# Splitting a state-space group at its scan, and a third weight buffer, in a hybrid encoder trunk

## The chip, the cores and the metric

The kernel runs on one core of a Trainium2 chip. The metric is the device time of one execution in microseconds (us); less is better. The program is built by a scheduler that fixes the order of instructions on each engine ahead of time; at run time each engine goes through its own list and waits on semaphores.

## The reference

One layer of an encoder on 3072 rows of 1024 columns (a sequence of 1024 and one of 2048), in float32. Cut to what matters:

```python
h = rmsnorm(x, norm_g);  proj = h @ w_in
u_a, v_a, z_a, x_b, z_b = split(proj)                 # five blocks of 1024 columns
y_a = gelu(u_a) * (w_s (x) layernorm(gelu(v_a)) + b_s) * silu(z_a)   # mixing in chunks of 128 rows
y   = s5_forward(x_b) + s5_backward(x_b) + d_skip * x_b    # 64 groups of 16 channels, 64 complex states
gy  = gelu(y);  gy = gy * sigmoid(gy @ w_glu + b_glu);  y_b = gy * silu(z_b)
out = rmsnorm(x + concat(y_a, y_b) @ w_out)
```

## The kernel before

All large products are made of float32 split into a high and a low part, three matmuls for each pair of tiles (`mm3`, lines 57 to 61): high by high, high by low, low by high. The rows are handled as three thirds (`th`) of 1024, each as two halves of 512 columns (`jh`).

There are four stages. The first (to 392 us) makes the block x_b for all thirds and the matrices of the S5 groups. The second (to 1727 us) makes the other four blocks of the input projection, third 2 first, then 0, then 1. The third makes the GLU product of the S5 branch in six halves, and the fourth the output projection.

In the second stage a third runs as follows. Four column blocks of v (`v_part`, line 506), each in four parts of 48 short matmuls into `acc`, with the layer norm statistics behind the last of them. Then eight feature blocks of z_b (`zb_op`), each in two half-steps of 24 matmuls, with eight matmuls of the mixing (`sv`) after each half-step. Then u and z_a by turns, 32 half-steps. A half-step's result leaves its PSUM buffer in two operations: a tanh or gelu on ScalarE (L541, L580), then a product on VectorE (L542, L582). Five PSUM buffers (tag `mm`) are shared by these and the mixing.

The weights of a sweep are in a tile `whl` of 1 MB. In third 2 it is loaded as float32 and split by ScalarE (L151) and GpSimd (L152), and stored; in the other thirds it is loaded ready made (`whl<-wc_d`, L146). The pool has two buffers. `next_w` asks for another one when the second half of a sweep is traced.

After each half-step or v part, `advance` (line 418) may take up to one more piece of the S5 generator `s5_groups` (line 1028): 128 pieces over 184 of these places, two pieces to a group. What a piece issues on ScalarE and on VectorE is queued behind the last eviction (`tail["S"]`, `tail["V"]`), which the gates of z_b, z_a and u set for both and the v parts for ScalarE alone; what it issues on TensorE isn't tied to anything.

The first piece of group g is `states(g)`: six matmuls `pb` (L59 to L61), two products with the cosine and sine table (L1108, L1109), a sum and a difference (L1110, L1111) into tile `b`, two scans over 64 partitions each (L1116), two products back (L1121, L1122), and four more operations (L1123 to L1126) that leave the states `h` in a high and a low part; then `prepare(g + 1)`, which splits that group's input `u` and matrices `mi` and `mo` (ScalarE at L1051; VectorE or GpSimd at L1052), and for two groups at once the angle tables (`tables`, `finish_tables`). The second piece is `outputs(g - 1)`: nine matmuls `py` and a gelu; then `decay(g + 1)` and `issue(g + 2)`, four loads on the SP queue. Tiles `h` and `mi` have two buffers; `u` and `mo` have three.

When the last group is done, `preload` gets the first two rows of `w_glu` and all eight tiles of the first GLU half (`gf`, `gh`) into the space that the groups used.

Of the kernel before, what the change touches and what calls it, by code (L numbers as in the profile page):

```python
# [21 lines left out]
P = 128  # L22
D = 1024
KT = 8
# [32 lines left out]
def mm3(nc, out, lh, ll, rh, rl, first, last):  # L57

    nc.tensor.matmul(out, lh, rh, start=first, stop=False)  # L59
    nc.tensor.matmul(out, lh, rl, start=False, stop=False)  # L60
    nc.tensor.matmul(out, ll, rh, start=False, stop=last)  # L61


def hybrid_encoder(ctx, tc, a, outs):
# [54 lines left out]

    halves, ready, staged = {}, [], []  # L120


# [16 lines left out]
    def split_w(hp):  # L139

        with tc.high_priority(offset=hp):
            if staged:
                n, wfs, view = staged.pop(0)
                w = wpool.tile([P, 2, KT, P], F32R, tag="whl", name="whl")
                if wfs is None:
# [36 lines left out]
    def sweep(pool, half, ops, after, hp=WHP):  # L182

        ws = [ready.pop(0) for _ in ops]
        for jh in range(2):
            for w, f in zip(ws, ops):
                ps = pool.tile([P, 512], F32, tag="mm", name="mm")
                h = half(jh)
                for kt in range(KT):
                    mm3(nc, ps, w[:, 0, kt], w[:, 1, kt], h[kt][:, 0], h[kt][:, 1], kt == 0, kt == KT - 1)  # L190
                if jh:
                    next_w(hp)
                f(jh, ps)
                after()
# [173 lines left out]
    with ExitStack() as p2:  # L368
# [6 lines left out]
        ps_b = p2.enter_context(tc.tile_pool(name="ps_b", bufs=1, space=PSUM))  # L375

        s5 = s5_groups(tc, spool, ps_b, small, kio, f8h, f8l, r8, xb_d, ks_d, mat_d, gy_d)
        done = [0, 0]
# [5 lines left out]
        def preload():  # L384
# [5 lines left out]
            elif len(wg) < 4:  # L390
# [7 lines left out]
                wg.append(w)  # L398
            elif len(g0) < KT:
                for kt in (len(g0), len(g0) + 1):  # L400
                    gf = wg[1].tile([P, 512], F32, name=f"gf{kt}")
                    dma(quad(gf), gy_half(0, kt))
                    gh = wg[1].tile([P, 2, 512], F32R, name=f"gh{kt}")
                    S.copy(gh[:, 0], gf)
                    V.tensor_tensor(gh[:, 1], gf, gh[:, 0].bitcast(F32), op=ALU.subtract)
                    g0.append((gf, gh))

        late = [[], []]
        tail = {}

# [40 lines left out]
        for th in (2, 0, 1):  # L451
# [53 lines left out]
            def v_part(acc, w, cb, q, jh):  # L505

                for cc in range(2):
                    ps = acc[jh][cc]
                    for i in range(2):
                        csl = slice(P * (2 * cc + i), P * (2 * cc + i) + P)  # L510
                        for t in range(4):
                            h, wh, wl = hs[jh][4 * q + t], w[:, 0, 2 * t:2 * t + 2], w[:, 1, 2 * t:2 * t + 2]

                            mm3(nc, ps[:, i], h[:, 0, csl], h[:, 1, csl], wh, wl, q == t == i == 0, q == i == 1 and t == 3)
                    if q:
# [112 lines left out]
    for kt in range(2, KT):  # L628
        wg.append(load_rows(a["w_glu"][0][P * kt:P * kt + P], wresB, yp, "f2k", 9))
    for kt in range(KT):  # L630
        z = e32t("z")
        dma(quad(z), zb_half(0, kt))
# [397 lines left out]
def s5_groups(tc, sp, ps, small, kio, f8h, f8l, r8, xb_d, ks_d, mat_d, gy_d):  # L1030
# [23 lines left out]
    def tables(g):  # L1054

        tb = sp.tile([P, 2, 2, KK], F32, tag="tab", name="tab", bufs=2)
        for q in range(2):
            sc, fr = f8h[:, g + q:g + q + 1], tb[:, q, 0]
            tmp = tb[:, q, 1]
            S.activation(tmp, kio, AF.Copy, scale=sc, bias=MAGIC)  # L1060
            S.activation(tmp, tmp, AF.Copy, bias=-MAGIC)
            V.scalar_tensor_tensor(fr, kio, sc, tmp, op0=ALU.mult, op1=ALU.subtract)
            V.scalar_tensor_tensor(fr, kio, f8l[:, g + q:g + q + 1], fr, op0=ALU.mult, op1=ALU.add)
        V.tensor_scalar(tb[:, :, 0], tb[:, :, 0], 0.5, -0.5, op0=ALU.min, op1=ALU.max)
        st["tab", g], st["tab", g + 1] = tb[:, 0], tb[:, 1]
        st["pair", g] = tb

    def finish_tables(g):
        tb = st.pop(("pair", g))
        S.activation(tb[:, :, 1], tb[:, :, 0], AF.Sin, scale=TWO_PI_LOW)  # L1070
        S.activation(tb[:, :, 0], tb[:, :, 0], AF.Abs)
        S.activation(tb[:, :, 0], tb[:, :, 0], AF.Sin, scale=-TWO_PI_LOW, bias=qpi)

# [13 lines left out]
    def prepare(g):  # L1087
        U, m1, m2 = st.pop(("raw", g))
        u = sp.tile([P, 2, KK], F32R, tag="u", name="u", bufs=3)
        mi = sp.tile([P, 2, 2, P], F32R, tag="mi", name="mi", bufs=2)  # L1090
        mo = sp.tile([P, 2, 3, P], F32R, tag="mo", name="mo", bufs=3)
# [3 lines left out]
        st[g] = u, mi, mo  # L1095

    def states(g):
        u, mi, mo = st[g]
        tb = st.pop(("tab", g))
        cs = tb[:, 0:1].to_broadcast(sh)  # L1100
        sn = tb[:, 1:2].to_broadcast(sh)

# [11 lines left out]
        for r, o, z in ((slice(0, 64), gp[:, 2:2 * KK + 2], (0, P)), (slice(64, 128), gp[:, 0:2 * KK], (P - 1, KK - 1))):  # L1114
            f = slice(None, None, 1 if r.start == 0 else -1)
            V.tensor_tensor_scan(o[r, f], dec[r, f], bf[r, f], 0.0, op0=ALU.mult, op1=ALU.add)  # L1116
            V.memset(gt[r, :, z[0]:z[1] + 1:z[1] - z[0]], 0.0)
        h = sp.tile([P, 2] + sh[1:], F32R, tag="h", name="h", bufs=2)
        h1 = sp.tile(sh, F32, tag="b1", name="h1")
# [33 lines left out]
    issue(0)  # L1153
    tables(0)
    prepare(0)
    finish_tables(0)
    decay(0)
    issue(1)
# [51 lines left out]
```

## Time and profile before

| what | value |
|---|---|
| median of 3 runs | 2536.09 us (2534.43 to 2537.3) |
| the profiled execution | 2535.16 us, of it a span of 2533.3 us |
| TensorE (matmul) busy | 2443.2 us of the span |
| VectorE busy | 1748.9 us |
| ScalarE busy | 959.0 us |
| GpSimd busy | 622.0 us |
| mean granted TensorE clock | 0.989 |

Busy time of TensorE is the union of its matmuls, which overlap one another in the pipeline, so a busy TensorE isn't one at its peak. A wait is idle time of an engine, put down to the instruction that ended it.

### The profile page before, as it was taken

How to read it: one execution, taken by the hardware profiler on the slowest of the kernel's cores; microseconds unless marked ns; L12 is line 12 of the kernel's file. 1: busy time of each engine (PE TensorE's matmuls, PEld its weight loads, DVE VectorE, ACT ScalarE, POOL GpSimd, SP SyncE). 2: the span in 40 equal slices, each digit the busy share in tenths (PEclk: the TensorE clock that was granted, in tenths of full speed). 3: DMA queues.
4: the chain of work that ended last, by engine and by line, in shares of the span. 5: the costliest groups of instructions: out<-in, count | busy, mean ns of one | idle time of the engine just before them, and what ended most of it. 6: DMA issues, size and time to landing. Idle time of an engine off the chain costs nothing.

```text
span 2533.3 us, 33967 instructions
## 1 busy us (share of the span) xinstructions
PE 2443.2 (96%) x12313; PEld 2080.2 (82%) x12313; DVE 1748.9 (69%) x2921; ACT 959.0 (38%) x1698; POOL 622.0 (25%) x623
## 2 busy tenths in 40 slices
PE   7899999989999899999999999999999999999998
PEld 5677779977888898888889788887888888888887
DVE  6898857899999979888887999764334433333332
ACT  5343334445554534444454444423223311111110
POOL 2579873344334302210130221001000200000000
PEclk9999999999999999999999999999999999999999
DMA  8565455445555533444453344455656632222220
GB/s 241 174 190 146 143 164 178 134 152 163 185 179 195 175 109 115 146 154 150 136 177 118 112 140 143 145 162 171 166 155 174 216 108 88 96 96 96 96 75 34
DMA packets 363017, 367.21 MB, mean 145 GB/s; under 512 B 40768, under 2 KB 308576, under 8 KB 350560
## 3 DMA queue, kind: packets, MB, share of 16 engines
q1 hardware_dynamic: 311008, 343.99, 43.0%
q10 hardware_dynamic: 51840, 21.04, 3.4%
q8 instruction: 97, 1.59, 0.3%
q14 instruction: 72, 0.59, 0.1%
HBM read 229.76 MB, written 135.20 MB: 144 GB/s over the span
## 4 chain that ended last, share of the span: by engine, by line
PE 69%; DVE 17%; POOL 3%; DMA 3%; issue 2%; ACT 1%; SPq 0%; ACTq 0%; DVEq 0%; POOLq 0%
PE mm L59 19%; PE mm L61 19%; PE mm L60 19%; DVE gt L1116 3%; PE acc L59 2%; PE acc L61 2%; PE acc L60 2%; DVE h L1122 1%; PE py L59 1%; PE py L61 1%; PE py L60 1%; DVE h L1121 1%; DVE v L479 1%; DMA hf<-hs_d 1%; PE s5b L1002 1%
## 5 line engine op out<-in xcount | busy, mean ns | idle before, releaser
L59 PE MATMUL mm<-w,yh 128*128 128x512 f32 x768 | 302.6, 394 | 0.0
L60 PE MATMUL mm<-w,yh 128*128 128x512 f32 x768 | 301.8, 393 | 0.0
L61 PE MATMUL mm<-w,yh 128*128 128x512 f32 x768 | 301.3, 392 | 0.0
L59 PE MATMUL mm<-hb,whl 128*128 128x512 f32 x704 | 278.3, 395 | 0.0
L59 PE MATMUL mm<-ha,whl 128*128 128x512 f32 x704 | 277.4, 394 | 0.9 <-DVE ha L287 0.8
L61 PE MATMUL mm<-ha,whl 128*128 128x512 f32 x704 | 275.4, 391 | 1.1 <-POOL whl L152 1.1
L60 PE MATMUL mm<-hb,whl 128*128 128x512 f32 x704 | 276.3, 393 | 0.0
L61 PE MATMUL mm<-hb,whl 128*128 128x512 f32 x704 | 276.3, 392 | 0.0
L60 PE MATMUL mm<-ha,whl 128*128 128x512 f32 x704 | 275.6, 391 | 0.0
L1116 DVE TENSOR_TENSOR_SCAN gt<-dec,b 64x768 f32<-64x768 f32 x128 | 230.8, 1803 | 3.1
L152 POOL TENSOR_TENSOR whl<-wf,whl 128x512 fp32r<-128x512 f32 x112 | 175.3, 1581 | 222.2 <-ACT whl L151 192.8
L1052 POOL TENSOR_TENSOR mi<-m,mi 128x256 fp32r<-128x256 f32 x64 | 60.9, 952 | 531.4 <-ACT mi L1051 531.4
L61 PEld LDWEIGHTS mm<-w,yh 128*128 128x128 f32 x768 | 144.3, 188 | 33.7
L59 PEld LDWEIGHTS mm<-w,yh 128*128 128x128 f32 x768 | 144.1, 188 | 33.2
L60 PEld LDWEIGHTS mm<-w,yh 128*128 128x128 f32 x768 | 144.2, 188 | 33.0
L695 DVE SCALAR_TENSOR_TENSOR yh<-yf,yh 128x512 fp32r<-128x512 f32 x96 | 66.8, 699 | 147.8 <-ACT yh L694 110.3
L724 DVE TENSOR_TENSOR xr<-xr,mm 128x512 f32<-128x512 f32 x48 | 33.0, 687 | 184.1 <-PE mm L61 184.1
L61 PEld LDWEIGHTS mm<-ha,whl 128*128 128x128 f32 x704 | 132.9, 189 | 29.5 <-POOL whl L152 1.6
L61 PEld LDWEIGHTS mm<-hb,whl 128*128 128x128 f32 x704 | 133.5, 190 | 28.2
L59 PEld LDWEIGHTS mm<-ha,whl 128*128 128x128 f32 x704 | 132.7, 189 | 27.1 <-DVE ha L287 1.5
L59 PEld LDWEIGHTS mm<-hb,whl 128*128 128x128 f32 x704 | 133.9, 190 | 25.5 <-DVE v L503 0.2
L60 PEld LDWEIGHTS mm<-hb,whl 128*128 128x128 f32 x704 | 133.8, 190 | 25.6 <-DVE hb L288 0.2
(243 smaller groups left out, 5922.3 us busy)
## 6 DMA issues: line engine op xcount, KB each, us to landing
whl<-wc_d SPq DMA_DIRECT2D x64, 1024.0 KB
wc_d<-whl SPq DMA_DIRECT2D x32, 1024.0 KB
wf<-in_w_in_dram SPq DMA_DIRECT2D x112, 256.0 KB
m<-mat_d SPq DMA_DIRECT2D x128, 128.0 KB
xb_d<-xo SPq DMA_DIRECT2D x24, 512.0 KB
U<-xb_d SPq DMA_DIRECT2D x64, 192.0 KB
gy_d<-gy SPq DMA_DIRECT2D x64, 192.0 KB
zb_d<-zb SPq DMA_DIRECT2D x24, 512.0 KB
```

The lines of the kernel that those rows point to most:

```text
L59: nc.tensor.matmul(out, lh, rh, start=first, stop=False)
L60: nc.tensor.matmul(out, lh, rl, start=False, stop=False)
L61: nc.tensor.matmul(out, ll, rh, start=False, stop=last)
L152: G.tensor_tensor(flat[:, 1, sl], wf, flat[:, 0, sl].bitcast(F32), op=ALU.subtract)
L479: V.tensor_scalar(v, v, rs[:, q:q + 1], nb[:, q:q + 1], op0=ALU.mult, op1=ALU.add)
L695: V.scalar_tensor_tensor(y[:, 1], yf, sc, y[:, 0].bitcast(F32), op0=ALU.mult, op1=ALU.subtract)
L724: V.tensor_tensor(x, x, t.ps[i], op=ALU.add)
L1002: T.matmul(pk[:, g], bm[:, i, g], pcl[i][:, g].rearrange("p j c -> p (j c)"), start=i == 0, stop=i == 1)
L1052: eng.tensor_tensor(t[:, 1], src, t[:, 0].bitcast(F32), op=ALU.subtract)
L1116: V.tensor_tensor_scan(o[r, f], dec[r, f], bf[r, f], 0.0, op0=ALU.mult, op1=ALU.add)
L1121: V.tensor_tensor(h1, gt, cs, op=ALU.mult)
L1122: V.tensor_tensor(h2, gt[:, ::-1], sn, op=ALU.mult)
```

## The change

A group's first piece now ends at the scan; the rest of the old `states` is a function `turn(g)` in the second piece, behind `outputs(g - 1)`. The preparation of the next group, its tables (half of a pair at a time) and the finishing of a pair move from the first piece to the second; `issue(g + 1)` stands at the end of the first piece in place of `issue(g + 2)` at the end of the second. `tail["T"]` holds the last matmul of a half-step or v part, so that the pieces' matmuls are queued behind it. `finish_tables` makes both angles first and then one Sin over both. Tiles `mi` and `h` have one buffer. The weights get a third buffer, a pool of its own in the second stage, taken by turns with the two others. To make room at the end of that stage, four of the eight `gf` tiles go through a staging tile, and are loaded a second time at the start of the GLU stage.

```diff
     halves, ready, staged = {}, [], []
+    pools = [wpool]
+    tail = {}
...
-                w = wpool.tile([P, 2, KT, P], F32R, tag="whl", name="whl")
+                w = pools[0].tile([P, 2, KT, P], F32R, tag="whl", name="whl")
+                pools.append(pools.pop(0))
...
+                    tail["T"] = mm3(nc, ps, w[:, 0, kt], w[:, 1, kt], h[kt][:, 0], h[kt][:, 1],
+                                    kt == 0, kt == KT - 1)
...
+        pools[:] = [p2.enter_context(tc.tile_pool(name="wpool3", bufs=1)), wpool, wpool]
+        next_w()
...
+                raw = stage_tile("gf").rearrange("p (a c) -> p a c", a=2) if len(g0) > 3 else None
                 for kt in (len(g0), len(g0) + 1):
-                    gf = wg[1].tile([P, 512], F32, name=f"gf{kt}")
+                    gf = wg[1].tile([P, 512], F32, name=f"gf{kt}") if kt < 4 else raw[:, kt % 2]
...
+                            tail["T"] = mm3(nc, ps[:, i], h[:, 0, csl], ...)     # in v_part
...
     for kt in range(KT):
+        if kt > 3:
+            g0[kt][0] = f32t("gf")
+            dma(quad(g0[kt][0]), gy_half(0, kt))
         z = e32t("z")
...
     def tables(g):
-        tb = sp.tile([P, 2, 2, KK], F32, tag="tab", name="tab", bufs=2)
-        for q in range(2):
-            ...
-        V.tensor_scalar(tb[:, :, 0], tb[:, :, 0], 0.5, -0.5, op0=ALU.min, op1=ALU.max)
+        if g % 2 == 0:
+            tb = sp.tile([P, 2, 2, KK], F32, tag="tab", name="tab", bufs=2)
+            ...
+        V.tensor_scalar(fr, fr, 0.5, -0.5, op0=ALU.min, op1=ALU.max)
     def finish_tables(g):
         tb = st.pop(("pair", g))
-        S.activation(tb[:, :, 1], tb[:, :, 0], AF.Sin, scale=TWO_PI_LOW)
+        S.activation(tb[:, :, 1], tb[:, :, 0], AF.Copy, scale=-1.0, bias=0.25)
         S.activation(tb[:, :, 0], tb[:, :, 0], AF.Abs)
-        S.activation(tb[:, :, 0], tb[:, :, 0], AF.Sin, scale=-TWO_PI_LOW, bias=qpi)
+        flat = tb.rearrange("p q i k -> p (q i k)")
+        S.activation(flat, flat, AF.Sin, scale=-TWO_PI_LOW, bias=qpi)
...
-        mi = sp.tile([P, 2, 2, P], F32R, tag="mi", name="mi", bufs=2)
+        mi = sp.tile([P, 2, 2, P], F32R, tag="mi", name="mi")
...
             V.memset(gt[r, :, z[0]:z[1] + 1:z[1] - z[0]], 0.0)
-        h = sp.tile([P, 2] + sh[1:], F32R, tag="h", name="h", bufs=2)
+    def turn(g):
+        u, mi, mo = st[g]
+        cs, sn = phase(g)
+        h = sp.tile([P, 2] + sh[1:], F32R, tag="h", name="h")
...
         states(g)
         store()
         if g < GRP - 1:
-            prepare(g + 1)
-        if g % 2 == 0 and g < GRP - 2:
-            tables(g + 2)
-        if g % 2 == 1 and g < GRP - 1:
-            finish_tables(g + 1)
+            issue(g + 1)
         yield
         if g:
             outputs(g - 1)
+        if g % 2 and g < GRP - 1:
+            tables(g + 2)
+        if g < GRP - 1:
+            prepare(g + 1)
+        turn(g)
+        if g % 2 and g < GRP - 1:
+            finish_tables(g + 1)
+        if g % 2 == 0 and g < GRP - 2:
+            tables(g + 2)
         if g < GRP - 1:
             decay(g + 1)
-        if g < GRP - 2:
-            issue(g + 2)
-        if g == GRP - 1:
+        else:
```

## Rows read from the trace of the kernel before

**Rows 1.** The page: the span, and VectorE's busy time, share and instructions.

```profile
span 2533.3 us, 33967 instructions
PE 2443.2 (96%) x12313; PEld 2080.2 (82%) x12313; DVE 1748.9 (69%) x2921; ACT 959.0 (38%) x1698; POOL 622.0 (25%) x623
```

**Rows 2.** TensorE's waits in the second stage: waiter, releaser, total us, times, longest.

```profile
PE sv L498 <- DVE zb L542: 23.5, 9, 5.8
PE acc L59 <- DMA whl<-wc_d: 11.0, 4, 7.5
PE acc L59 <- ACT hb L444: 2.2, 1, 2.2
```

**Rows 3.** Windows: length, PE, PEld, DVE, ACT, POOL busy, clock, DMA share, GB/s.

```profile
498.00:643.00 145.00, 129.60 (x622) 111.31 (x621) 141.35 (x194) 73.35 (x141) 67.16 (x47) 0.94 0.51 162
643.00:840.00 197.00, 197.00 (x907) 167.85 (x906) 189.61 (x235) 102.40 (x169) 75.45 (x52) 1.00 0.56 184
959.00:1090.00 131.00, 124.61 (x619) 107.38 (x618) 120.89 (x194) 65.78 (x124) 34.74 (x28) 0.99 0.44 138
1400.00:1533.00 133.00, 126.54 (x622) 108.96 (x621) 120.84 (x189) 67.14 (x125) 34.84 (x28) 0.97 0.43 135
```

**Rows 4.** Windows at half clock in the second stage (seven of them), and their sum.

```profile
842.80:853.00 10.20, 4.63 (x22) 4.67 (x23) 6.92 (x9) 4.82 (x10) 5.51 (x4) 0.50 0.76 275
sum 37.40, PE 26.98 PEld 24.16 DVE 33.64 ACT 19.80 POOL 16.09; mean PE 3.85 PEld 3.45 DVE 4.81 ACT 2.83 POOL 2.30
```

**Rows 5.** Timeline of VectorE at 1440 us: start, us, engine, line, operation, tiles.

```profile
1440.46 0.95 DVE L1122 TENSOR_TENSOR h<-gt,tab 128x768 f32<-128x768 f32 x1
1441.33 0.68 DVE L542 SCALAR_TENSOR_TENSOR zb<-zb,mm 128x512 f32<-128x512 f32 x1
```

**Rows 6.** Windows of tiles b and h alone; lines of VectorE in the second stage.

```profile
385.00:1690.00 1305.00, 423.67 (x384) 0.99 0.46 150
385.00:1690.00 1305.00, 78.46 (x384) 68.71 (x384) 327.15 (x384) 0.99 0.46 150
L1062 DVE SCALAR_TENSOR_TENSOR tab<-kio,f8h,tab 128x384 f32<-128x384 f32 x61 | 44.5, 733 | 1.5 <-ACT tab L1061 0.6
L1052 DVE TENSOR_TENSOR u<-U,u 128x384 fp32r<-128x384 f32 x62 | 37.6, 607 | 24.5 <-PE pb L61 21.0 <-ACT u L1051 3.5
```

**Rows 7.** Timelines of the SP queue and of VectorE at the change of thirds.

```profile
841.69 0.36 SPq L440 DMA_DIRECT2D hf<-hs_d  x1
842.15 0.42 SPq L146 DMA_DIRECT2D whl<-wc_d  x1
...
840.94 0.68 DVE L445 TENSOR_TENSOR ha<-hf,ha 128x512 fp32r<-128x512 f32 x1
...
864.84 0.68 DVE L445 TENSOR_TENSOR hb<-hf,hb 128x512 fp32r<-128x512 f32 x1
```

**Rows 8.** Timelines of TensorE and VectorE: pb, and the gate of the half-step before.

```profile
614.61 0.39 PE L59 MATMUL pb<-u,mi 128*128 128x384 f32 x1
...
614.62 0.68 DVE L542 SCALAR_TENSOR_TENSOR zb<-zb,mm 128x512 f32<-128x512 f32 x1
...
1571.33 0.34 PE L59 MATMUL pb<-u,mi 128*128 128x384 f32 x1
...
1569.05 0.68 DVE L582 TENSOR_TENSOR v<-v,mm 128x512 f32<-128x512 f32 x1
```

**Rows 9.** Timelines of VectorE and GpSimd: one operation beside GpSimd, and alone.

```profile
500.55 1.65 DVE L1111 TENSOR_TENSOR b<-b,b 128x384 f32<-128x384 f32 x1
...
498.94 2.84 POOL L152 TENSOR_TENSOR whl<-wf,whl 128x512 fp32r<-128x512 f32 x2
...
827.82 0.55 DVE L1111 TENSOR_TENSOR b<-b,b 128x384 f32<-128x384 f32 x1
```

**Rows 10.** Timelines of the SP queue and of TensorE at the GLU's start.

```profile
1748.98 6.89 SPq L643 DMA_DIRECT2D gf<-gy_d  x8
...
1761.60 0.50 PE L59 MATMUL mm<-gh,w 128*128 128x512 f32 x1 [0.60 <-ACT t L674]
```

**Rows 11.** Lines of ScalarE in the second stage: the second Sin of a pair.

```profile
L1072 ACT ACTIVATE tab<-tab,qpi 128x768 f32<-128x768 f32 x31 | 29.1, 939 | 0.9
```

More of the change, by code (lines that the diff above doesn't have):

```diff
@@ L60, in mm3 @@
     nc.tensor.matmul(out, lh, rl, start=False, stop=False)
-    nc.tensor.matmul(out, ll, rh, start=False, stop=last)
+    return nc.tensor.matmul(out, ll, rh, start=False, stop=last)
 def hybrid_encoder(ctx, tc, a, outs):
@@ L189, in sweep @@
                 for kt in range(KT):
-                    mm3(nc, ps, w[:, 0, kt], w[:, 1, kt], h[kt][:, 0], h[kt][:, 1], kt == 0, kt == KT - 1)
+                    tail["T"] = mm3(nc, ps, w[:, 0, kt], w[:, 1, kt], h[kt][:, 0], h[kt][:, 1],
+                                    kt == 0, kt == KT - 1)
                 if jh:
@@ L405, in preload @@
                     V.tensor_tensor(gh[:, 1], gf, gh[:, 0].bitcast(F32), op=ALU.subtract)
-                    g0.append((gf, gh))
+                    g0.append([gf, gh])
         late = [[], []]
-        tail = {}
+        tail.clear()
         def flush():
@@ L512, in v_part @@
                             h, wh, wl = hs[jh][4 * q + t], w[:, 0, 2 * t:2 * t + 2], w[:, 1, 2 * t:2 * t + 2]
-                            mm3(nc, ps[:, i], h[:, 0, csl], h[:, 1, csl], wh, wl, q == t == i == 0, q == i == 1 and t == 3)
+                            tail["T"] = mm3(nc, ps[:, i], h[:, 0, csl], h[:, 1, csl], wh, wl, q == t == i == 0, q == i == 1 and t == 3)
                     if q:
@@ L1054, in tables @@
     def tables(g):
-        tb = sp.tile([P, 2, 2, KK], F32, tag="tab", name="tab", bufs=2)
-        for q in range(2):
[L1058 to L1063, printed above, removed]
-        V.tensor_scalar(tb[:, :, 0], tb[:, :, 0], 0.5, -0.5, op0=ALU.min, op1=ALU.max)
-        st["tab", g], st["tab", g + 1] = tb[:, 0], tb[:, 1]
-        st["pair", g] = tb
+        if g % 2 == 0:
+            tb = sp.tile([P, 2, 2, KK], F32, tag="tab", name="tab", bufs=2)
+            st["tab", g], st["tab", g + 1] = tb[:, 0], tb[:, 1]
+            st["pair", g] = tb
+        sc, tb = f8h[:, g:g + 1], st["tab", g]
+        fr, tmp = tb[:, 0], tb[:, 1]
+        S.activation(tmp, kio, AF.Copy, scale=sc, bias=MAGIC)
+        S.activation(tmp, tmp, AF.Copy, bias=-MAGIC)
+        V.scalar_tensor_tensor(fr, kio, sc, tmp, op0=ALU.mult, op1=ALU.subtract)
+        V.scalar_tensor_tensor(fr, kio, f8l[:, g:g + 1], fr, op0=ALU.mult, op1=ALU.add)
+        V.tensor_scalar(fr, fr, 0.5, -0.5, op0=ALU.min, op1=ALU.max)
     def finish_tables(g):
         tb = st.pop(("pair", g))
-        S.activation(tb[:, :, 1], tb[:, :, 0], AF.Sin, scale=TWO_PI_LOW)
+        S.activation(tb[:, :, 1], tb[:, :, 0], AF.Copy, scale=-1.0, bias=0.25)
         S.activation(tb[:, :, 0], tb[:, :, 0], AF.Abs)
-        S.activation(tb[:, :, 0], tb[:, :, 0], AF.Sin, scale=-TWO_PI_LOW, bias=qpi)
+        flat = tb.rearrange("p q i k -> p (q i k)")
+        S.activation(flat, flat, AF.Sin, scale=-TWO_PI_LOW, bias=qpi)
     st = {}
@@ L1095, in prepare, with phase @@
         st[g] = u, mi, mo
+    def phase(g):
+        tb = st["tab", g]
+        return tb[:, 0:1].to_broadcast(sh), tb[:, 1:2].to_broadcast(sh)
     def states(g):
         u, mi, mo = st[g]
-        tb = st.pop(("tab", g))
-        cs = tb[:, 0:1].to_broadcast(sh)
-        sn = tb[:, 1:2].to_broadcast(sh)
+        cs, sn = phase(g)
         pb = ps.tile([P, 2, 512], F32, tag="pb", name="pb")[:, :, 0:KK]
@@ L1117, in states @@
             V.memset(gt[r, :, z[0]:z[1] + 1:z[1] - z[0]], 0.0)
-        h = sp.tile([P, 2] + sh[1:], F32R, tag="h", name="h", bufs=2)
+    def turn(g):
+        u, mi, mo = st[g]
+        cs, sn = phase(g)
+        h = sp.tile([P, 2] + sh[1:], F32R, tag="h", name="h")
         h1 = sp.tile(sh, F32, tag="b1", name="h1")
@@ L1154, in s5_groups @@
     tables(0)
+    tables(1)
     prepare(0)
@@ L1157, in s5_groups @@
     decay(0)
-    issue(1)
     for g in range(GRP):
```

## The prediction, made before the changed kernel was run

> **What bounds the kernel now.** I read the page first: TensorE is busy 2443.2 of 2533.3 us [rows 1], so the most that any schedule can win is its idle time and what it loses at half clock. The windows by stage come next. The last two stages have TensorE busy almost without a break, and the change touches them only at the GLU's start; the first stage isn't touched. So the second stage decides, and in it TensorE's waits are the view to read. Nearly all of them are of two kinds [rows 2]. In the first, TensorE stands at a mixing product `sv`, whose PSUM buffer is held by a half-step of z_b that VectorE hasn't gated yet: 23.5 us in nine waits. In the second it stands at the first products of a v part, and waits for weights (11.0 us) or for the input half (2.2 us). With four waits of 1 to 2 us more the view gives 42.4 us.
>
> The windows at half clock belong to these waits: each one begins within a few us of a wait, and in all seven of them the granted clock is 0.50, the level of 1.2 GHz, against 1.00 (2.4 GHz) before. TensorE was busy for 26.98 us of their 37.40 us [rows 4], and half of that busy time, 13.5 us, is the loss. So a wait of 1 us costs about 1.3 us, and 42.4 + 13.5 = 55.9 us is all that there is to win, 2.2%.
>
> Why is VectorE late? It is nearly full. In z_b of the first third done it is busy 141.35 of 145 us while TensorE idles 15.4 us, and in the u and z_a that follow 189.61 of 197 us; in z_b of the other two thirds it is busy 120.89 of 131 and 120.84 of 133 us, and TensorE idles there 6.4 and 6.5 us [rows 3]. Part of the lateness is mere order. At 1441.33 us a z_b gate runs that ScalarE had released some 10 us before, and ahead of it stands the group's chain, products into `b`, scans, then products into `h` [rows 5].
>
> **The change, part by part.** *The split.* Of a group, VectorE's work up to the scan is 423.67/64 = 6.6 us, and behind it 327.15/64 = 5.1 us; with `u` (0.61) and the tables, two operations of about 0.73 us and a clamp, the whole is some 14 us, all in the first piece [rows 6]. After the change the first piece has 6.6 us, and the second 5.1 + 0.6 + 1.8 = 7.5 us. The second is queued behind the last gate traced, so a gate stands behind at most half a group. In the two later thirds VectorE has 10 and 12 us of idle time in the z_b stretch [rows 3], enough to take the chain later. TensorE loses there 6.4 and 6.5 us of idle time and about 1.3 and 4.0 us by the clock column (length times what is missing to 1.00) [rows 3], 7.7 and 10.5 us. I take 5 and 6.5 us of these, not all, since part of each stretch's backlog is the layer norm of the second half, which precedes the gate before and after.
>
> In the first third VectorE is idle for only 145 - 141.35 = 3.7 us of z_b and 197 - 189.61 = 7.4 us of u and z_a, where TensorE has no idle time to give [rows 3]. The work is the same after the change, so TensorE can't win more than these 11 us there, whatever the order, although it loses 15.4 us and up to 8.7 us of clock. Besides, the pieces of the v parts aren't bound to any gate of this third, so that the first wait, of 5.8 us, has a chain ahead of it that the change doesn't bind either. I take 7, from between 0 and 11.
>
> What fills VectorE in that third is also GpSimd: the same operation of 384 columns takes 1.65 us beside a weight split and 0.55 us alone [rows 9]. The Trainium skill (SBUF — State Buffer, section "SBUF: two separate sides") says that VectorE and GpSimd share one pair of ports as an exclusive lock, where the loser is blocked for the whole instruction. The row agrees. By that rule the split saves nothing where GpSimd fills the rest, and the sum would have 0 in place of the first third's 7 us.
>
> *The third weight buffer.* At the change from third 2 to third 0 the load `whl<-wc_d` is issued at 842.15 us, right behind a load `hf` at 841.69 that had waited for VectorE's `ha` at 840.94, and TensorE idles 7.5 us until it lands [rows 2, 7]. With a third buffer the first of the two weights is asked for one sweep earlier. The second still needs a buffer of the last sweep, and the next halves still come through four staging tiles, the last piece of `hb` as late as 864.84 + 0.68 us [rows 7]. So I count 6 of the 7.5 + 4.63/2 = 9.8 us at this place [rows 2, 4], 3 of the other 5.7 us of such waits (11.0 + 2.2 - 7.5) [rows 2], and 1 us for one wait for GpSimd's split in the first third: 10 us, with 4 (only the waits behind later weights) and 17 (all) as bounds.
>
> Gain: 5 + 6.5 + 7 + 10 = 28.5 us.
>
> *The later preparation.* Before, `u` and `mi` of the next group were split a whole group ahead of its `pb`; now they are split in the piece just before, behind the gate of that half-step on VectorE. What is queued behind a `pb` that waits is everything: the next half-step's products. The trace doesn't show this wait, so I bound it. I took each `py` to `pb` distance of z_b, u and z_a (47 of them) and placed `u` behind the old time of the gate: gate end, 0.8 us for the two mixing additions or for the product of z_a, 1.6 us of tables where the group is odd, 0.55 us. In 12 of 47 it is late, first by 3.7 us (gate until 615.30, `pb` at 614.61), last by 1.3 us (gate until 1569.73, `pb` at 1571.33) [rows 8], in all 44.2 us. That is the upper end, since the late gates themselves stand behind chains that the change takes away, and since `u` is ready earlier than the tables and may go ahead of them. The lower end is 0: the scheduler can place `pb` some products later. Below 0 there is nothing, for no work leaves. I take 5 us, near the lower end, since most of the 44 us are at the gates that gain most.
>
> *The single buffers.* `h` is overwritten in the piece that issues `py` of the old `h` first, and the copy into `h` comes behind the tables and four other VectorE operations, 4 us and more, while `py` takes 1.6 us at the end of the half-step. `mi` was read by `pb` one piece earlier. Cover: those operations; if it fails, it is the wait of the part above. 0 us. The loads of `issue` move by half a group on the SP queue, with the same distance of one piece to their use: 0 us.
>
> *ScalarE and the clamps.* A pair's second Sin took 0.94 us over 768 columns [rows 11]; over 1536 it lies between 0.94 and twice that, and Copy in place of the first Sin is about even, so up to 0.9 us more for a pair, on an engine that is busy only half of each stretch [rows 3]. 32 clamps more on VectorE are small. I take 1 us together, between 0 and 4, for gates that stand behind the longer run.
>
> *The second load of `gf`.* At the GLU's start eight `gf` loads keep the SP queue for 6.9 us [rows 10]; four more of the same kind come ahead of them, 3.4 us, and share nine buffers with them, the last of which come free only when the gates of the first GLU half are done. TensorE's idle there was 0.6 us [rows 10]. The slack in front of the next half's products hides most of it: 2 us, between 0 and 6.
>
> Sum: 2535.2 us (the profiled execution, a span of 2533.3 [rows 1] and 1.9 around it; it is 0.9 us under the median) - 28.5 + 5 + 1 + 2 = 2514.7, so 2515 us. With the terms at their bounds the forecast's own range is 2500 to 2529.
>
> **The rivals.**
>
> *Slower: TensorE waits at `pb`.* The preparation is too close to its use, and the wait at `sv` turns into one at `pb` in all three thirds. It decides from (28.5 - 3)/1.3, about 20 us of such waits, fewer than half of the 44 us above. With 33 us it gives 2535.2 - 28.5 + 3 + 33 x 1.3 = 2553. For it: 12 late distances, at gates up to 10 us behind. Against it: 35 distances have 1 to 10 us to spare. The Trainium skill (Trainium Kernel Development and Optimization, section "Best Practices") says to double-buffer for performance, which speaks against the single buffers; no row before can show it, as both tiles had two.
>
> *No change: VectorE is the bound wherever TensorE waits.* Then the order gives nothing, each gate served earlier makes a later one late, and only the weight buffer is won: 2535.2 - 10 + 8 = 2533. This is also the case in which the scheduler leaves the chains where they were. For it: VectorE's 97% in the first third. Against it: the 10 and 12 us of idle time in the others [rows 3].
>
> *Much faster:* all waits and half-clock windows go, with 5 us of new cost: 2535.2 - 55.9 + 8 = 2487. It needs VectorE to be less stretched in the first third.
>
> **How the numbers follow.** The forecast has 0.50, the slower rival 0.22, no change 0.15, much faster 0.13. The range takes in the forecast, no change, the better part of the much faster case and that part of the slower rival that lies just past its turning point: 2488 to 2549. A measurement of this kernel tells about 0.2%, 5 us, from no change. Faster: 0.50 + 0.13 and a little of the no-change case, 0.65; within: 0.13; slower: 0.22.
>
> **What would show it.** Right: the waits of `sv` for the gate of z_b fall from 23.5 us to some 8, the 7.5 us wait at the change of thirds to about 2, the half-clock windows to about half their sum, and VectorE's share in z_b of the first third stays at 97%. Waits of `pb` for `u` or `mi` sum to 5 us at most, and none appears at `py`. Wrong: a row of `pb` waiting for VectorE or GpSimd over 20 us, or waits at the first products of the GLU's second half of several us, or `sv` waits in the first third that go away altogether.

## The result and the profile after

The changed kernel takes 2569.49 us (median; 2567.37 to 2573.25) against 2535.98 us of the kernel before on the same chip: a ratio of 1.0134, 95% interval 1.0116 to 1.0152. The forecast was 2515 us, the range ended at 2549 us, and the sign was wrong. The profiled execution is 2569.38 us, 34.2 us above that of before.

The page's span, busy times and instructions, to be read against [rows 1]:

```profile
span 2567.5 us, 34008 instructions
PE 2458.2 (96%) x12313; PEld 2091.4 (81%) x12313; DVE 1773.1 (69%) x2953; ACT 978.8 (38%) x1701; POOL 659.5 (26%) x623
```

TensorE's matmuls are as many as before and are busy 15.0 us longer. TensorE's waits after (waiter, releaser, total us, times, longest), to be read against [rows 2]:

```profile
PE sv L507 <- DVE zb L551: 31.3, 13, 7.7
PE pb L60 <- DVE u L1064: 9.2, 4, 6.3
PE acc L61 <- DVE hb L454: 4.3, 2, 3.5
PE acc L61 <- POOL ha L454: 3.7, 1, 3.7
PE acc L61 <- POOL hb L454: 2.4, 2, 1.6
```

The weights' row, 11.0 us, is gone: the third buffer does what it says. In its place the input halves hold up the v parts (4.3 + 3.7 + 2.4 = 10.4 us), and `pb` waits for `u`. The row that was to fall to 8 us, `sv` behind the gate of z_b, has grown from 23.5 to 31.3 us.

One of the eleven windows of the second stage at half clock, and their sum (columns as in [rows 4]):

```profile
519.20:529.40 10.20, 5.25 (x15) 4.35 (x16) 9.82 (x27) 8.40 (x12) 1.27 (x1) 0.50 0.59 191
...
sum 64.60, PE 52.17 PEld 47.25 DVE 60.55 ACT 34.42 POOL 23.89; mean PE 4.74 PEld 4.30 DVE 5.50 ACT 3.13 POOL 2.17
```

TensorE was busy for 52.17 us at a granted clock of 0.50 (1.2 GHz), 26.98 us before: half of the difference, 12.6 us, is lost by that. TensorE's idle time in the second stage, the shortest waits included, went from 42.6 to 59.5 us. 16.9 + 12.6 = 29.5 of the 34.2 us are found.

The stretches of z_b after, to be read against [rows 3] (first, second and last third):

```profile
504.00:652.00 148.00, 125.13 (x594) 106.99 (x593) 136.19 (x190) 75.80 (x139) 68.22 (x46) 0.93 0.48 154
...
985.00:1117.00 132.00, 123.67 (x596) 106.63 (x596) 120.08 (x193) 67.05 (x123) 38.99 (x28) 0.95 0.40 129
1433.40:1562.70 129.30, 122.29 (x598) 105.39 (x597) 118.00 (x184) 66.42 (x122) 38.24 (x26) 0.96 0.40 124
```

VectorE has 11 to 12 us of idle time in each of these z_b stretches, in the first third too, where it had 3.7. It isn't fuller than before there; it is held up more, and by ScalarE. VectorE's waits in z_b of the first third, before:

```profile
DVE zb L542 <- ACT zb L541: 1.6, 1, 1.6
```

After, 9.4 of its 11.8 us of idle time:

```profile
DVE v L512 <- ACT v L511: 4.8, 2, 2.4
DVE zb L551 <- ACT zb L550: 4.6, 3, 2.0
```

What ScalarE itself waits for, over the whole kernel, before:

```profile
ACT dec L1131 <- DVE gt L1116: 108.0, 40, 9.5
ACT L1070 <- DVE tab L1064: 19.6, 7, 4.7
ACT zb L541 <- PE mm L61: 125.9, 37, 6.6
```

After:

```profile
ACT dec L1152 <- DVE gt L1132: 128.5, 29, 10.5
ACT tab L1083 <- DVE tab L1078: 90.3, 26, 5.4
ACT zb L550 <- PE mm L61: 128.3, 30, 8.2
```

Before, ScalarE waited 7 times for the clamp of a table; now it stands there 26 times. And it finds fewer half-steps still at work when it comes to evict them: 30 of the 48 of z_b instead of 37. A case from the timelines, the longest delay of an eviction, of ScalarE first (start, us, engine, line, operation, tiles, idle time before):

```profile
513.51 0.94 ACT L1152 ACTIVATE dec<-keep,r 128x768 f32<-128x768 uint8 x1 [7.15 <-DVE gt L1132]
514.36 1.12 ACT L154 CAST whl<-wf 128x512 fp32r<-128x512 f32 x2
520.90 0.84 ACT L1083 ACTIVATE tab<-tab 128x768 f32<-128x768 f32 x1 [5.42 <-DVE tab L1078]
521.78 0.84 ACT L1084 ACTIVATE tab<-tab 128x768 f32<-128x768 f32 x1
522.53 0.58 ACT L550 ACTIVATE zb<-mm 128x512 f32<-128x512 f32 x1
523.13 1.28 ACT L1086 ACT_TABLE_LOAD   x1
524.42 1.57 ACT L1086 ACTIVATE tab<-tab,qpi 128x1536 f32<-128x1536 f32 x1
...
527.06 1.28 ACT L550 ACT_TABLE_LOAD   x1
528.36 0.60 ACT L550 ACTIVATE zb<-mm 128x512 f32<-128x512 f32 x1
```

The clamp that it waited for, and the gate that came late, on VectorE:

```profile
520.47 0.35 DVE L1078 TENSOR_SCALAR tab<-tab 128x384 f32<-128x384 f32 x1
...
523.32 0.68 DVE L551 SCALAR_TENSOR_TENSOR zb<-zb,mm 128x512 f32<-128x512 f32 x1
```

TensorE, at the end of the half-step whose eviction comes at 522.53, and at the wait:

```profile
509.13 0.39 PE L61 MATMUL mm<-ha,whl 128*128 128x512 f32 x1
...
524.06 0.58 PE L507 MATMUL sv<-wsT,vh 128*128 128x256 f32 x1 [7.74 <-DVE zb L551]
```

The half-step was done at 509.52 us. ScalarE was idle for most of the time from there to 520.90, first for the scan that frees the decay's tile, then for the clamp, and its eviction, which could have run at any moment of it, stood behind them in the list: 13.0 us late. The next half-step's eviction, at 528.36, stands behind the table load, the Sin and the load back.

TensorE's wait at that place, 7.74 us, can't be put down to this delay: VectorE worked without a break until its gate at 523.32, and at the same product TensorE waits in kernels that have no such delay, 5.84 us before, 7.60 us in e7 and, with an eviction only 0.24 us late, in e5:

```profile
519.43 0.58 PE L507 MATMUL sv<-wsT,vh 128*128 128x256 f32 x1 [8.31 <-DVE zb L551]
```

A wait that neither the kernel before nor e5 has is this one in the second third, of ScalarE, VectorE and TensorE in turn:

```profile
1038.05 0.85 ACT L1083 ACTIVATE tab<-tab 128x768 f32<-128x768 f32 x1 [4.76 <-DVE tab L1078]
...
1043.97 0.60 ACT L550 ACTIVATE zb<-mm 128x512 f32<-128x512 f32 x1
...
1044.60 0.69 DVE L551 SCALAR_TENSOR_TENSOR zb<-zb,mm 128x512 f32<-128x512 f32 x1 [4.05 <-ACT zb L550]
...
1045.35 0.58 PE L507 MATMUL sv<-wsT,vh 128*128 128x256 f32 x1 [3.92 <-DVE zb L551]
```

That half-step was done at 1034.62 us. ScalarE stood idle for the clamp, then made the Copy, the Abs, the table load, the Sin and the load back, and the eviction was 9.35 us late; VectorE stood at its gate for 4.05 us, and TensorE waited 3.92 us for that gate. Only five of TensorE's waits, 8.3 us together, end with a VectorE operation that had itself just waited for ScalarE; the way from the late evictions to the other waits isn't traced one by one.

### The profile page after: what moved, and what is told of

The parts are those of the page before. It is cut to its first block, busy times and chain, and to the rows that moved or that the text cites. A ratio compares the mean times of both kernels' runs of the same rounds, so it can differ in the third digit from the quotient of the medians.

```text
span 2567.5 us, 34008 instructions
## 1 busy us (share of the span) xinstructions
PE 2458.2 (96%) x12313; PEld 2091.4 (81%) x12313; DVE 1773.1 (69%) x2953; ACT 978.8 (38%) x1701; POOL 659.5 (26%) x623
## 3 DMA queue, kind: packets, MB, share of 16 engines
q1 hardware_dynamic: 313120, 345.04, 42.6%
## 4 chain that ended last, share of the span: by engine, by line
PE 53%; DVE 5%; DMA 1%; ACT 1%; issue 1%; SPq 0%; POOL 0%; DVEq 0%; ACTq 0%
PE mm L59 15%; PE mm L61 15%; PE mm L60 15%; PE acc L61 1%; PE acc L60 1%; PE acc L59 1%; DVE gt L1132 1%; PE py L59 1%; PE py L61 1%; PE py L60 1%; DMA gf<-gy_d 1%; PE sv L507 0%; PE pb L59 0%; PE pb L61 0%; PE pb L60 0%
## 5 line engine op out<-in xcount | busy, mean ns | idle before, releaser
L1132 DVE TENSOR_TENSOR_SCAN gt<-dec,b 64x768 f32<-64x768 f32 x128 | 239.0, 1867 | 3.5
L1064 POOL TENSOR_TENSOR mi<-m,mi 128x256 fp32r<-128x256 f32 x64 | 73.5, 1148 | 507.3 <-ACT mi L1063 498.8
```

Source lines behind the costliest of these rows:

```text
L1064: eng.tensor_tensor(t[:, 1], src, t[:, 0].bitcast(F32), op=ALU.subtract)
```

## The experiments

The theory: the tables' work in the second piece holds up ScalarE's evictions, and costs what the other parts win and more. The rivals: the later preparation (the one of the prediction), the third weight buffer with its second load, and the split itself.

For each run I also worked out, from the timelines of TensorE and ScalarE, how long after its last product each of the 192 results of the second stage is evicted (144 half-steps, 48 results of v): the lateness. The least is 0.04 us in every kernel.

| kernel | us | ratio (95% interval) | sum of lateness, us | over 3 us |
|---|---|---|---|---|
| before | 2535.98 | | 86.7 | 8 |
| after | 2569.49 | 1.0134 (1.0116 to 1.0152) | 362.7 | 43 |
| e1: tables by pairs, finishing in the next first piece | 2524.00 | 0.9943 (0.9927 to 0.9960) | 244.1 | 32 |
| e2: after, two weight buffers | 2572.75 | 1.0140 (1.0125 to 1.0155) | 333.5 | 42 |
| e3: before, tables late | 2618.99 | 1.0320 (1.0305 to 1.0335) | 452.3 | 53 |
| e4: before, split alone | 2528.05 | 0.9968 (0.9956 to 0.9979) | 72.5 | 6 |
| e5: after, tables at their old places | 2520.76 | 0.9932 (0.9918 to 0.9947) | 81.7 | 11 |
| e6: before, one Sin | 2537.20 | 0.9997 (0.9987 to 1.0006) | 92.8 | 7 |
| e7: e5, preparation at its old place | 2516.98 | 0.9914 (0.9899 to 0.9929) | 108.2 | 11 |
| e8: e5, two weight buffers | 2530.05 | 0.9975 (0.9966 to 0.9984) | 62.1 | 8 |
| e9: after, only the clamps early | 2542.93 | 1.0020 (1.0010 to 1.0029) | 171.8 | 23 |
| e10: e7, products not queued | 2517.44 | 0.9921 (0.9902 to 0.9939) | 103.1 | 10 |
| e11: e9 without the Sin | 2529.37 | 0.9970 (0.9958 to 0.9983) | 92.4 | 10 |
| e12: after without the Sin | 2522.42 | 0.9951 (0.9936 to 0.9966) | 166.0 | 21 |

**The tables elsewhere (e1).** Of the changed kernel's loop, only the tables' and the finishing's places are moved:

```diff
             issue(g + 1)
+        if g % 2 and g < GRP - 1:
+            finish_tables(g + 1)
         yield
...
-        if g % 2 and g < GRP - 1:
-            tables(g + 2)
...
-        if g % 2 and g < GRP - 1:
-            finish_tables(g + 1)
         if g % 2 == 0 and g < GRP - 2:
             tables(g + 2)
+            tables(g + 3)
```

> The changed kernel with one part undone: the tables of both groups of a pair are made in the second piece of the even group, and the pair is finished (Copy, Abs, Sin) in the first piece of the odd group, as before the change. Theory A (ScalarE stands in its order at the pair's Copy, waiting for VectorE's clamp made in the same piece, and evictions queue behind it: 90.3 us of such waits, evictions 2.0 us late on average against 0.4 before): the waits fall under 30 us, the evictions' mean lateness to under 1 us, and the time by 20 us or more, to 2540 to 2550. Theory B (the loss comes from preparing u and mi in the piece just ahead of their use, 9.2 us of waits at pb, and from what follows): the time stays within 5 us of 2569.

2524.0 us: 45 us less than after, and faster than before. But ScalarE's waits for the clamp, which I had taken for the measure of it, grew, while those for the scan fell from 128.5 us:

```profile
ACT tab L1083 <- DVE tab L1078: 121.8, 26, 10.9
...
ACT dec L1152 <- DVE gt L1132: 45.7, 13, 8.9
```

So the place counts, and the waits for the clamp aren't what it counts by. That was the part of the theory that had to be taken back.

**Two weight buffers (e2).** The third pool, and with it the staging of `gf` and its second load, are taken out of the changed kernel:

```diff
-        pools[:] = [p2.enter_context(tc.tile_pool(name="wpool3", bufs=1)), wpool, wpool]
-        next_w()
...
-        if kt > 3:
-            g0[kt][0] = f32t("gf")
-            dma(quad(g0[kt][0]), gy_half(0, kt))
```

> The changed kernel without the third weight buffer and without the second load of gf, all else as changed. By the prediction's terms the buffer wins 10 us and the second load costs 2, so without them 2577. Theory A says nothing else: if the buffer is what moved ScalarE's and GpSimd's splits ahead of evictions, the time falls below 2560 instead.

2572.75 us, 3 us above after, with intervals that overlap: the buffer isn't the cause of the loss, and in this kernel it is worth little.

**Only the late tables (e3).** The kernel before, with `tables` by halves of a pair and both it and `finish_tables` in the second piece (and the one Sin); no split, no third buffer, the preparation where it was:

```diff
-        if g % 2 == 0 and g < GRP - 2:
-            tables(g + 2)
-        if g % 2 == 1 and g < GRP - 1:
-            finish_tables(g + 1)
         yield
         if g:
             outputs(g - 1)
+        if g % 2 and g < GRP - 1:
+            tables(g + 2)
+            finish_tables(g + 1)
+        if g % 2 == 0 and g < GRP - 2:
+            tables(g + 2)
```

> The kernel before with one part of the change alone: tables half a pair at a time, the pair finished in the second piece of the odd group by Copy, Abs and one Sin; the groups are not split, weights and buffers as before. Theory A: ScalarE waits for the clamp as in the changed kernel (60 us or more), evictions are over 1.5 us late on average, and the time rises by 15 us or more, to over 2551. Theory B: 2536, within 5 us.

2618.99 us, 81 us slower than before, from this part alone. I had expected the sign, not the size. ScalarE's and TensorE's waits in it:

```profile
ACT dec L1133 <- DVE gt L1118: 197.1, 42, 11.0
ACT tab L1071 <- DVE tab L1066: 132.8, 28, 7.0
...
PE sv L498 <- DVE zb L542: 35.1, 13, 6.6
PE acc L59 <- DMA whl<-wc_d: 21.5, 4, 7.9
```

Both of ScalarE's rows are larger than after the whole change, and so is the lateness, 452 us. The finishing follows its clamp here at once, with nothing between them. And not only evictions are held up: TensorE waits 39.5 us for weights (12.1 before), 8.5 us of them for ScalarE's own splits of the weights.

**The split alone (e4).** The kernel before with the work behind the scan in the second piece:

```diff
         if g:
             outputs(g - 1)
+        turn(g)
```

> The kernel before with the split alone: the operations behind the scan stand in the second piece, behind the out products; tables, preparation, loads, weights and buffers as before. By the prediction's terms the split wins 18.5 us: about 2518. If VectorE is the bound wherever TensorE waits, 2536, within 5 us. Theory A allows either; it excludes a loss of over 10 us.

2528.05 us, 9.8 us faster than the kernel before beside it (2537.86; by the interval 5 to 11 us). The split is a gain, of about half the forecast 18.5 us.

**The tables at their old places (e5).** The whole change but for the places of `tables` (both of a pair in the first piece of an even group) and `finish_tables` (in that of an odd one):

```diff
             issue(g + 1)
+        if g % 2 == 0 and g < GRP - 2:
+            tables(g + 2)
+            tables(g + 3)
+        if g % 2 and g < GRP - 1:
+            finish_tables(g + 1)
         yield
```

> The changed kernel with the tables at their old places altogether: both groups' tables in the first piece of the even group, the pair finished in the first piece of the odd group. Theory A in its revised form (what costs is not the length of ScalarE's wait for the clamp, 121.8 us in the kernel with the tables half undone, but that evictions stand behind it): with the tables made a whole piece earlier the waits for the clamp fall under 40 us, evictions are under 0.6 us late on average, and the time is 2510 to 2522. If the tables' VectorE work in the first piece delays the gates again (first piece 6.6 + 3.3 us): 2525 to 2535.

2520.76 us. So the tables' places are worth 2569.49 - 2520.76 = 48.7 us of the changed kernel (51 us by the two ratios), and the lateness falls from 363 to 82 us. Its waits:

```profile
ACT tab L1083 <- DVE tab L1078: 12.0, 7, 3.4
...
PE sv L507 <- DVE zb L551: 20.2, 7, 8.3
PE pb L60 <- DVE u L1064: 6.8, 3, 3.1
```

The waits of `sv` don't go to 8 us even now; I come back to that.

**One Sin instead of two (e6).** The kernel before with the new form of `finish_tables` at the old place:

```diff
-        S.activation(tb[:, :, 1], tb[:, :, 0], AF.Sin, scale=TWO_PI_LOW)
+        S.activation(tb[:, :, 1], tb[:, :, 0], AF.Copy, scale=-1.0, bias=0.25)
         S.activation(tb[:, :, 0], tb[:, :, 0], AF.Abs)
-        S.activation(tb[:, :, 0], tb[:, :, 0], AF.Sin, scale=-TWO_PI_LOW, bias=qpi)
+        S.activation(flat, flat, AF.Sin, scale=-TWO_PI_LOW, bias=qpi)
```

> The kernel before with the form of the finishing alone: Copy, Abs and one Sin over 1536 columns in place of Sin, Abs, Sin, at the old place. Theory A in its revised form (the place costs, not the form): 2536, within 6 us. If the longer Sin, some 0.6 us more for each of 32 pairs, stands in front of evictions: 2545 or more, half-way to the kernel with the late tables.

A ratio of 0.9997: the form costs nothing where it stood before. It is the place.

**The preparation at its old place too (e7).** e5 with `prepare` and `issue` where the kernel before has them; the single buffers stay:

```diff
-            issue(g + 1)
+            prepare(g + 1)
...
-        if g < GRP - 1:
-            prepare(g + 1)
         turn(g)
...
+        if g < GRP - 2:
+            issue(g + 2)
```

> The kernel with the tables at their old places, and besides with preparation and loads at their old places, so that of the change the split, the queueing behind the last matmul, the single buffers, one Sin and the third weight buffer remain. If the later preparation costs what the prediction took for it (5 us, waits at pb): 3 to 8 us under the kernel with the tables alone put back, and the waits at pb under 2 us. If it costs nothing, or if u in the first piece delays the gates: the same within 3 us or slower.

2516.98 us, 3.8 us less than e5, and the waits of `pb` are gone. It is the fastest kernel of the study.

**e5 with two weight buffers (e8).** The edit of e2, made to e5.

> The kernel with the tables at their old places, without the third weight buffer and the second load of gf. By the prediction's terms the buffer wins 10 us and the second load costs 2: 8 us more than with it, and a wait of 7 us or more for the weights at the change of thirds. If what the buffer frees turns into a wait for the input halves: within 3 us.

2530.05 us: with the tables out of the way the third buffer is worth 9.3 us, three times what it was worth in e2. TensorE's long wait at the change of thirds is back (7.8 us), though the trace puts it down to a late eviction of z_a and not to the weights.

**The clamp or the finishing (e9).** Two accounts of the 48.7 us were left. A1: ScalarE waits for angles that VectorE makes just ahead of their use. A2: the finishing, Copy, Abs, a table load, the Sin and a load back for the next function, is one long run in a bad place. e9 is the changed kernel with the tables' work in the first piece of an even group, and the finishing still in the second piece of an odd one:

```diff
             issue(g + 1)
+        if g % 2 == 0 and g < GRP - 2:
+            tables(g + 2)
+            tables(g + 3)
         yield
...
-        if g % 2 and g < GRP - 1:
-            tables(g + 2)
...
-        if g % 2 == 0 and g < GRP - 2:
-            tables(g + 2)
```

> The changed kernel with the tables' VectorE work put back alone: both groups' tables in the first piece of the even group, the pair still finished in the second piece of the odd group. It tells ScalarE's waiting from ScalarE's work. Theory A1 (the waiting for a clamp made in the same piece): the clamp is then a whole piece old, waits for it under 20 us, evictions under 0.6 us late on average, 2518 to 2526. Theory A2 (the run of Copy, Abs, table load and Sin, 4.6 us, standing ahead of evictions in the second piece, whatever it waits for): evictions 1 us late or more, 2540 or more.

2542.93 us, between the two: 26.6 us go with the early clamps (and the tables' other operations, which move with them), and 22 us stay. ScalarE's waits for the clamp are down to 1.6 us.

**The products not queued (e10).** e7 with no `tail["T"]`:

```diff
-                    tail["T"] = mm3(nc, ps, w[:, 0, kt], w[:, 1, kt], h[kt][:, 0], h[kt][:, 1],
+                    mm3(nc, ps, w[:, 0, kt], w[:, 1, kt], h[kt][:, 0], h[kt][:, 1],
```

> The fastest kernel so far (tables, preparation and loads at their old places) without the queueing of a piece's matmuls behind the last matmul of the step. The prediction gave it no cost and no gain, since pb and py stood at the ends of steps before as well: the same within 3 us. If matmuls of a piece then go ahead of products that are needed sooner: slower by 5 us or more.

2517.44 us, no difference to e7: the queueing of the pieces' products neither costs nor wins anything.

**Without the Sin (e11, e12).** e9 and the changed kernel, each without the one instruction that makes the run long (the tables then hold the angles):

```diff
-        S.activation(flat, flat, AF.Sin, scale=-TWO_PI_LOW, bias=qpi)
```

> The kernel of e9 (tables' clamps early, finishing in the second piece) without the Sin over 1536 columns; the tables then hold the angles themselves, so the values of the S5 branch are others. With the Sin go its two table loads: 1.58 + 2 x 1.28 us of the 5.8 us that ScalarE works in one go for a pair (rows of e9). Theory A2 (what is left of the loss in e9, 22 us over the 2520.8 of the kernel with the tables at their old places, is that this run stands ahead of a half-step's eviction): the time falls by about 4.15/5.8 of 22, 16 us, to 2527, and by up to the whole 22 to 2521, if a shorter run misses the evictions altogether; the mean lateness of the evictions falls from 0.83 us to under 0.4. Rival B (the 22 us come from VectorE or GpSimd, on which the late finishing makes the products with the tables wait, or from another order of the gates): the run's length doesn't count, 2538 to 2543.

> The changed kernel as it is, late clamps and late finishing, without the Sin over 1536 columns and so without its two table loads; the tables hold the angles, so the values of the S5 branch are others. If waiting for the clamp and the run behind it are two costs that add up (27 and 22 us of the 48.7 us), 16 to 22 us go: 2547 to 2553. If the waiting alone matters: 2565 to 2570. If the run alone matters, and the waiting only because the run stands behind it: 2521 to 2535.

| | Sin in | Sin left out |
|---|---|---|
| clamp late, finishing late | after: 2569.49 | e12: 2522.42 |
| clamp early, finishing late | e9: 2542.93 | e11: 2529.37 |

e11 loses 13.6 of the 22 us that stayed in e9; 8.6 us over e5 remain, which no run explains. The rival named before it, that VectorE waits for the finished tables, doesn't fit the waits: VectorE's products with a table wait 10.1 us for ScalarE's work on a table after the change, but 12.2 us in e5 and 12.9 us in e9.

e12 says most. It is 47.1 us faster than after, with the clamps as late as they were; its waits on ScalarE:

```profile
ACT dec L1151 <- DVE gt L1131: 98.9, 23, 8.8
ACT tab L1083 <- DVE tab L1078: 98.1, 27, 5.5
```

Waiting for the clamp takes 98.1 us here, more than the 90.3 us of after, and costs nothing that can be seen; without the Sin the late clamp is no slower than the early one (2522 and 2529 us). So the two costs don't add up, as I had put it in the expectations: the wait costs where the long run stands behind it. Nor is that enough by itself: in e1 the same Sin stands behind still longer waits, in a first piece, and the kernel is 3 us slower than e5. The timeline of ScalarE in e12, at the place shown above:

```profile
514.23 0.84 ACT L1083 ACTIVATE tab<-tab 128x768 f32<-128x768 f32 x1 [5.46 <-DVE tab L1078]
515.10 0.84 ACT L1084 ACTIVATE tab<-tab 128x768 f32<-128x768 f32 x1
515.85 0.58 ACT L550 ACTIVATE zb<-mm 128x512 f32<-128x512 f32 x1
...
517.37 0.62 ACT L550 ACTIVATE zb<-mm 128x512 f32<-128x512 f32 x1
```

The same wait of 5.4 us, and then two evictions within 1.5 us. After the change there were 5.8 us between the same two (522.53 and 528.36).

What the Sin brings with it is more than itself. Lines of ScalarE over the whole of the changed kernel:

```profile
L1086 ACT ACTIVATE tab<-tab,qpi 128x1536 f32<-128x1536 f32 x32 | 50.6, 1580 | 0.4
L1086 ACT ACT_TABLE_LOAD x31 | 39.8, 1283 | 0.6
...
L550 ACT ACT_TABLE_LOAD x17 | 21.8, 1283 | 0.3
L1163 ACT ACT_TABLE_LOAD x14 | 18.0, 1283 | 0.2
L589 ACT ACT_TABLE_LOAD x13 | 16.7, 1283 | 0.2
L528 ACT ACT_TABLE_LOAD x5 | 6.4, 1283 | 3.5 <-DMA xb_d<-xo 3.4
```

80 table loads in these lines, of which only one, at L528, is left in e12; 79 x 1.283 + 50.6 = 152 us, and ScalarE's busy time is indeed 154 us less there. The Trainium skill (ScalarE: Activation LUTs, section "Table sets: the hidden batching unit") advises to batch activations by their table set, since each switch costs a load; e12 is in line with it. Before the change the second stage had 77 of them, so that it isn't their number that changed, but where they fall.

What stays open: in e12 ScalarE also has 154 us less to do everywhere, and I made no run without the Sin at the old places, so that how much of the 47 us is tied to the place isn't settled by e12 alone. e5, which has every Sin and no loss, says that the place does most of it. Nor does lateness alone set the time: e1 has 244 us of it and takes 2524 us, e9 has 172 us and takes 2543, and e12, with 166 us, takes 2522. Which evictions can be late without harm isn't settled; that it depends on how many PSUM buffers are free at the time was only argued.

## Why the prediction was wrong

**The step that failed** is *ScalarE and the clamps*, 1 us with 4 as its upper end, for "an engine that is busy only half of each stretch". Measured, the tables' new places cost 48.7 us (after against e5), or 81 us in e3. The busy share was right, and it still is about half (75.80 of 148 us in the first z_b stretch). The inference was wrong: a ScalarE that stands idle at the head of its list, waiting for VectorE, can't evict, so its idle time was no cover for what was put in front of the evictions (lateness 363 us after, 82 us in e5).

How the 48.7 us reach TensorE is shown in part. Its idle time in the second stage is 59.5 us after and 31.4 us in e5. Of these 28 us, 11.1 are at `sv` and 2.3 at half-steps, behind z_b's gates; 11.7 are at the v parts, which wait for the splits of the input halves (none in e5); 2.4 are at `pb`. So the evictions are one way and the input halves another, and how much of the second comes from ScalarE isn't separated.

The numbers to read stood in the trace of the kernel before: ScalarE's waits, 108.0 us for the scan and 19.6 us for the tables, both in the same view as [rows 11]. I asked, of the step that is moved, what its work costs, but not what it waits for and who is queued behind it; I did ask that for `pb`.

**The sum, term by term**, against the forecast:

| term | forecast, us | measured, us | from |
|---|---|---|---|
| split | -18.5 | -9.8 | e4 |
| third weight buffer (with the second `gf` load) | -10 + 2 | -9.3 | e8 to e5 |
| later preparation | +5 | +3.8 | e5 to e7 |
| ScalarE and clamps | +1 | +48.7 | after to e5 |

2535.2 - 9.8 - 9.3 + 3.8 + 48.7 = 2568.6, and the profiled execution took 2569.4 us. The last term is counted back from the changed kernel itself, so what the sum tests is the first three: 2519.9, against 2520.8 us for e5. With the failed term at its forecast value of 1 us it would be 2521. The range that the prediction gave for its own terms, 2500 to 2529 us, doesn't follow from their bounds: with all of them at one end (first third 11 or 0, buffer 17 or 4, preparation 0 or 44, ScalarE 0 or 4, `gf` 0 or 6) they give 2496 to 2574.

**The split** was over-sized, and in the place where the prediction named a reason against itself. The table gives the lengths of stretches, from the start of the first product of one to that of the next (z_b and the u and z_a behind it together), for kernels with two weight buffers:

| third | before | e4 | e8 | forecast gain |
|---|---|---|---|---|
| first done | 349.9 | 350.0 | 354.5 | 7 |
| second | 332.6 | 329.5 | 329.2 | 5 |
| last | 326.4 | 321.6 | 319.8 | 6.5 |

The two later thirds gave 3 and about 5 to 7 us, where 5 and 6.5 were forecast; the first third gave nothing, and in e8 it is 4.6 us longer. (The profiled execution of e4 is 6 us above that kernel's median, so that its lengths are rather too long.) I had taken 7 from between 0 and 11 us there; it was 0. With the third buffer as well, in e7, the first third takes 340.4 us; the buffer without the split wasn't run, so whether the split has a part in those 9 us isn't told. By the Trainium skill's rule on the lock between VectorE's and GpSimd's ports (SBUF — State Buffer, section "SBUF: two separate sides") the sum had 0 in its place, and the trace of e4 agrees with the consequence; that the lock is the cause no run here shows. That third also holds most of the `sv` waits that stay in e5 and e7, 16.2 of 20.2 us and 15.0 of 20.9.

**The third weight buffer** and **the second load of `gf`** came out as forecast (8 and 9.3 us together); the GLU stage took 265.7 us before and 265.8 after, so that the load shows no cost where 2 us were forecast. In the changed kernel itself the gain was eaten: the wait for weights went, and those for the input halves, whose splitting begins on ScalarE, took 10.4 us in its place.

**The rival that ended slower**, `pb` waiting for `u`, gave 2553 us from 33 us of such waits. There were 9.2 us of them, and undoing the later preparation is worth 3.8 us (e7): the forecast's 5, not the rival. The sentence of the Trainium skill on double-buffering (Trainium Kernel Development and Optimization, "Best Practices") was weighed with this rival; e7 keeps the single buffers of `h` and `mi` and is the fastest kernel, but no run gives these tiles their second buffers back alone, so that what the single ones cost isn't told.

**The signs.** `sv` waits were to fall to 8 us, and are 31.3; the half-clock windows were to halve, and their sum went from 37.4 to 64.6 us; `pb` waits were to be 5 us at most, and are 9.2; at `py` there was to be none, and there is one of 0.7. VectorE's share in the first z_b stretch was to stay at 97%, and is 92%: it is busy 136.19 us there instead of 141.35, in a stretch 3 us longer. Only the wait for weights behaved. No sign that I had named looked at ScalarE.

## What to carry to other kernels

The idle time of an in-order engine is no cover for extra work while the engine waits at the head of its list: ask, for each instruction that is moved, what it will wait for and what is queued behind it, and read that engine's own waits, not its busy share. A long run on the engine that empties PSUM (here a Copy, an Abs and a Sin with two table loads, 5.8 us) is to be timed in each place that it can have: in the first piece of an odd group it cost no more than the two Sins that it replaced (e6), and 3 us more with its input late (e1); in the second piece it cost 22 us more with its input early (e9) and 49 us with it late. What makes the second piece so dear was only argued. When a change has several parts, time each alone: here three that were worth 15 us together were hidden by a fourth that cost 49.

## What the hardware showed that I had not expected

- A change of function on ScalarE costs a load of 1.283 us in every one of the 80 cases, and the next instruction follows within 0.01 us (523.13 + 1.28, then 524.42). The Trainium skill (ScalarE: Activation LUTs, section "What ACT_TABLE_LOAD costs") adds about 1.38 us of drain to each switch; the rows of this case don't show it.
- The Sin over 1536 columns took 1.58 us, 1.7 times that over 768 [rows 11].
- What a wait of TensorE brings with it at half clock isn't a fixed share: 42.6 us of idle time in the second stage came with 13.5 us lost at a granted clock of 0.50 (1.2 GHz) before (0.32 us for each), 59.5 us with 26.1 us after (0.44), and in e12 only 28.2 us with 12.5 us (0.44). The prediction's factor of 1.3 for a wait fits the kernel before; after the change it is 1.44.
